# A two-layer hybrid block on one core: squares, a convolution tap and two affine maps from VectorE to ScalarE, and fewer table instructions

## The chip, the core and the metric

The kernel runs on one core of a Trainium2 chip. A core has TensorE (PE in the rows; its weight loads are PEld), VectorE (DVE), ScalarE (ACT), GpSimd (POOL), SyncE (SP), which here issues the transfers, and 16 DMA engines. Each engine works through its own queue of instructions in a fixed order and stops where an instruction has to wait for another engine. The metric is the device time of one execution in microseconds.

## The reference, cut to what matters

Two layers of one trunk run over 512 latent tokens and 256 context tokens of width 1024. In each layer a normalized, modulated input is projected once, its columns are split among three mixers (S5, a complex diagonal state space; gated DeltaNet, GDN; RWKV-7), and the outputs are joined, projected and added. Then comes an MLP with a squared ReLU. The context part of layer 1 has no output and no MLP.

```python
h = rmsnorm(x, norm_mlp[layer]) * (1.0 + sc2) + sh2
x = x + gt2 * (jnp.square(jax.nn.relu(h @ w1)) @ w2)

# GDN: five taps over the sequence, per channel, on the q, k and v columns
qkv = jax.nn.silu(centred_dwconv(p[..., :3 * W], conv_w))

# RWKV-7
k_dir = k[:, :, None, :] * (1.0 + (iclr - 1.0) * k_a)
yn = ((y - mean) * lax.rsqrt(var + RWKV_GN_EPS)).reshape(B, L, RWKV_WIDTH) * ln_w + ln_b

# S5: powers and products of complex numbers, from which the scan's tables are made
a_bar = jnp.exp(A * dt)
coef = (a_bar - 1.0) / A
```

## The kernel before

**Layout and products.** Features lie on the 128 partitions and tokens on the free axis, 512 for the latent part (LAT) and 256 for the context part (CTX). Every large product is made in three fp32r matmuls: the high parts of both operands, the low part of the weight, the low part of the activation (`product`, L296). A block of weights arrives by DMA (`wl`, four buffers), ScalarE rounds it to the high part (L272, `wh`, three buffers), and GpSimd or VectorE subtracts for the low part (L273, `wo`, two buffers); in the LAT MLPs that is GpSimd alone. Activations are split likewise: ScalarE casts (L284), VectorE subtracts (L285).

**Banks.** PSUM results go through named banks. Tag `d`, which the dense products, the convolution and the S5 tables share with other work, has two.

**Stages.** From 0 to some 34 us inputs, weights and modulations are worked on. The S5 tables of layer 0 (`s5_tables`) are begun before the first dense product at 63 us. Then come the input projections of both parts with the convolutions in them (to about 420 us), the GDN and RWKV chains, the S5 mixer, the output projections, the CTX MLP (about 900 to 1300 us) and the LAT MLP of layer 0 (about 1330 to 1960 us, with the tables and some of the input projections of layer 1 between its products). Layer 1's mixers follow, and the last MLP (about 2633 to 2990 us).

**Order.** The order on each engine isn't written out. Code carries priorities (chains first, then reads, preparation, S5, and the dense products), and a scheduler that runs its own timeline sets the order of each queue from these and its own estimates. So an instruction that goes to another engine can move other rows too.

**MLP (`back`).** For each of eight blocks of features, four dense products go to bank `d`; each is read by a ReLU on ScalarE (L1140), squared on VectorE (L1141), cast on ScalarE (L284) and subtracted on VectorE (L285). Then eight products over this block are added to the stream by VectorE (L1150), which frees the bank. There are 96 squares, 64 of 512 columns and 32 of 256.

**Convolution (`conv`).** ScalarE copies the bank into a padded tile (L467), VectorE multiplies the first tap (L470) and adds four more (L472), ScalarE takes the tanh (L473). It runs 33 times. The bank is free when L467 is done.

**Affine maps.** In the RWKV preparation VectorE does `kd * hka + omka` (L1571, 24 times), and in its readout `yc * ln_w + ln_b` (L1749, 9 times).

**Complex products.** `cmul` (L527) makes one of six instructions. `s5_tables` calls it on VectorE for the coefficients, the powers, the tables `f` and, in loops over `p`, for the power table `e` and the squarings whose small tiles have the tag `t5`; later, per group pair, on GpSimd and on VectorE.

Of the kernel before, what the change touches and what calls it, by code (L numbers as in the profile page):

```python
# [11 lines left out]
AF = mybir.ActivationFunctionType  # L12
# [14 lines left out]
        "td": (24, 4), "tp": (24, 4), "tq": (24, 4), "tg": (24, 4), "tr": (24, 4), "t5": (8, 6), "wc": (24, 4),  # L27
# [62 lines left out]
class Kern:  # L90
# [370 lines left out]
    def conv(self, ps, i, n, col):  # L461
# [65 lines left out]
    def cmul(self, eng, o, x, y, t, conj=False):  # L527

        tt = eng.tensor_tensor
        (orr, oi), (xr, xi), (yr, yi), (t0, t1) = o, x, y, t  # L530
        tt(t0, xr, yr, OP.mult)
        tt(t1, xi, yi, OP.mult)
        tt(orr, t0, t1, OP.add if conj else OP.subtract)
        tt(t0, xi, yr, OP.mult)
        tt(t1, xr, yi, OP.mult)
        tt(oi, t0, t1, OP.subtract if conj else OP.add)

    def s5_tables(self, l, col, tags):
# [81 lines left out]
        br, bi = new(), new()  # L620
# [8 lines left out]
        co = (new(), new())  # L629
        self.cmul(v, co, (br, bi), (are, aim), sc[1:3], conj=True)  # L630
        for c in co:
            tt(c, c, q, OP.mult)
        pr, pi = new(9), new(9)
# [4 lines left out]
        t0, t1 = self.s(64), self.s(64)  # L638
        for p in (1, 2, 4):
            sh = lambda a: a[:, :16 * p].rearrange("p (m c) -> p m c", c=16)  # L640
            bc = lambda a: a[:, p:p + 1].to_broadcast([P, p, 16])
            self.cmul(v, (pr[:, p + 1:2 * p + 1], pi[:, p + 1:2 * p + 1]), (pr[:, 1:p + 1], pi[:, 1:p + 1]),
# [12 lines left out]
        wr, wi = new(), new()  # L655
        stt(wr, cm, 1.0, m, OP.add, OP.mult)
        tt(wi, s, m, OP.mult)
# [15 lines left out]
        t = [tw[:, 256 * i:256 * i + 256].rearrange("p (d g c) -> p d g c", d=2, g=8) for i in range(2)]  # L673
        for d in range(2):
            bb = [s5bc[:, 128 * i:128 * i + 128].rearrange("p (g c) -> p g c", c=16) for i in range(2)]
            cc = [c[:, 8 * d:8 * d + 8].unsqueeze(2).to_broadcast([P, 8, 16]) for c in co]
            self.cmul(v, [x[:, d] for x in f], bb, cc, [x[:, d] for x in t])
# [5 lines left out]
        for d in range(2):  # L683
# [8 lines left out]
            ur, ui = wr[:, 8 * d:8 * d + 8], wi[:, 8 * d:8 * d + 8]  # L692
            p = 1
            while p < 96:
# [3 lines left out]
                self.cmul(v, [x[:, :, at(p, p + k)] for x in e], [x[:, :, at(0, k)] for x in e], (bc(ur), bc(ui)), (sh(t0), sh(t1)))  # L698
# [1215 lines left out]
```

## Time and profile before

| | us |
|---|---|
| median of three runs | 3021.07 |
| the three runs | 3020.94, 3021.07, 3024.71 |
| the profiled execution, its own time | 3012.89 |
| its span | 3011.1 |
| TensorE busy | 2663.1 (88%) |
| VectorE busy | 1725.7 (57%) |
| GpSimd busy | 1122.3 (37%) |
| ScalarE busy | 1096.4 (36%) |

The rows are from the profiled execution, which took 8.18 us less than the median of the runs; 1.8 us of its time lie outside the span. A share of busy time is a mean over stages with different limits, so the table alone doesn't tell what a shorter queue on one engine is worth. For that one reads which wait of TensorE ended last, and on whom.

### The profile page before, as it was taken

The page shows a single profiled execution, that of the slowest core. Times are in us where ns is not written, and L with a number is a line of the kernel's source. Part 1 is how long each engine was busy: PE and PEld are TensorE (multiplying, and loading weights), DVE is VectorE, ACT ScalarE, POOL GpSimd, SP SyncE. Part 2 cuts the span into 40 slices and gives each one's busy share as a digit, 9 for nine tenths or more (in the row PEclk, how much of TensorE's full clock was granted, in tenths as well). Part 3 has the DMA queues.
Part 4 walks back from the last instruction along what each step waited for, and adds up shares of the span by engine and source line. Part 5 has one row for each costly group of instructions (what it writes and reads, how often), then busy time and mean ns, then how long its engine had stood idle before and what let it go on. Part 6 is the DMA issues. An engine that isn't in the chain of part 4 may idle for free. (4 is left out here: it accounts for less than half of the span.)

```text
span 3011.1 us, 54432 instructions
## 1 busy us (share of the span) xinstructions
PE 2663.1 (88%) x20052; PEld 2044.2 (68%) x20052; DVE 1725.7 (57%) x4281; ACT 1096.4 (36%) x2250; POOL 1122.3 (37%) x1275
## 2 busy tenths in 40 slices
PE   5889998876899999987889999888888889799998
PEld 2767875653668888776667677667655567478776
DVE  7654875764657667558777543547656453333333
ACT  3344443231434443455323323443323232233332
POOL 2432434433232220323447444344343422244443
PEclk8789998676889999977999999889899768699999
DMA  5345546544645544443344233265466532023322
GB/s 207 95 156 175 153 125 197 158 142 136 206 147 173 141 152 137 147 141 109 88 103 142 94 91 107 90 196 157 135 206 193 163 101 87 29 86 96 95 94 85
DMA packets 324650, 401.65 MB, mean 133 GB/s; under 512 B 142880, under 2 KB 173472, under 8 KB 324384
## 3 DMA queue, kind: packets, MB, share of 16 engines
q1 hardware_dynamic: 324384, 398.18, 43.1%
q8 instruction: 158, 2.59, 0.4%
q14 instruction: 108, 0.88, 0.1%
HBM read 300.70 MB, written 88.90 MB: 129 GB/s over the span
## 5 line engine op out<-in xcount | busy, mean ns | idle before, releaser
L296 PE MATMUL d<-page,wh 128*128 128x512 f32 (+1 forms) x5024 | 1425.3, 367 | 57.3 <-DVE page L1150 22.0
L296 PEld LDWEIGHTS d<-page,wh 128*128 128x128 f32 x5024 | 918.9, 196 | 232.7 <-DVE page L1150 26.6
L296 PE MATMUL d<-page,wo 128*128 128x512 f32 (+1 forms) x2512 | 917.7, 366 | 13.7 <-POOL wo L273 7.4
L273 POOL TENSOR_TENSOR wo<-wl,wh 128x512 fp32r<-128x512 f32 (+1 forms) x357 | 481.0, 1348 | 670.0 <-PE d L296 520.9
L272 ACT CAST wh<-wl 128x512 fp32r<-128x512 f32 (+1 forms) x590 | 360.2, 616 | 553.9 <-PE d L296 391.1
L296 PEld LDWEIGHTS d<-page,wo 128*128 128x128 f32 x2512 | 492.8, 196 | 91.5 <-POOL wo L273 10.7
L273 DVE TENSOR_TENSOR wo<-wl,wh 128x512 fp32r<-128x512 f32 (+1 forms) x233 | 167.4, 720 | 105.1 <-PE d L296 41.5
L1150 DVE SCALAR_TENSOR_TENSOR page<-d,mod,page 128x512 f32<-128x512 f32 (+1 forms) x192 | 124.7, 658 | 161.9 <-PE d L296 161.4
L1141 DVE TENSOR_TENSOR s<-s 128x512 f32<-128x512 f32 (+1 forms) x96 | 82.3, 858 | 158.8 <-ACT s L1140 155.8
L371 DVE TENSOR_TENSOR solve<-solve 128x30 f32<-128x30 f32 (+4 forms) x360 | 138.1, 384 | 53.9 <-issue 46.2
L373 DVE TENSOR_TENSOR solve<-solve 128x30 f32<-128x30 f32 (+4 forms) x360 | 150.7, 419 | 8.0
L1493 POOL TENSOR_TENSOR g<-g,gates 64x128 f32<-64x128 f32 x120 | 59.4, 495 | 185.1 <-DVE g L1498 164.6
L923 PE MATMUL d<-wl,sc 128*32 128x512 f32 x320 | 109.5, 717 | 14.3 <-DMA wl<-in_mod_w_dram 12.8
L285 DVE TENSOR_TENSOR page<-s,page 128x512 fp32r<-128x512 f32 (+1 forms) x118 | 92.4, 785 | 41.5 <-ACT page L284 41.1
L1140 ACT ACTIVATE s<-d 128x512 f32<-128x512 f32 (+1 forms) x96 | 50.6, 527 | 165.8 <-PE d L296 165.6
L284 ACT CAST page<-s 128x512 fp32r<-128x512 f32 (+1 forms) x118 | 64.0, 547 | 92.9 <-DVE s L1141 74.1
L472 DVE SCALAR_TENSOR_TENSOR s<-s,ncol,s 128x512 f32<-128x512 f32 (+1 forms) x132 | 93.8, 713 | 2.8
L1727 PE MATMUL rc<-page,page 128*64 128x64 f32 x464 | 86.0, 273 | 2.0 <-DMA page<-dr 2.0
L1616 PEld LDWEIGHTS p<-page,page 64*128 64x128 f32 x576 | 74.3, 211 | 19.5 <-issue 8.1
L1616 PE MATMUL p<-page,page 64*128 64x128 f32 (+1 forms) x576 | 86.5, 310 | 0.7 <-POOL page L1590 0.7
L1704 DVE TENSOR_TENSOR page<-page,rc 64x128 f32<-64x128 f32 x144 | 40.9, 284 | 78.8 <-PE rc L1702 73.5
L481 PE MATMUL p<-consts,page 128*128 128x128 f32 x348 | 63.7, 306 | 24.6 <-ACT page L1642 9.6
(461 smaller groups left out, 3977.9 us busy)
## 6 DMA issues: line engine op xcount, KB each, us to landing
wl<-in_w_dram SPq DMA_DIRECT2D x384, 256.0 KB, 2.7
wl<-in_mod_w_dram SPq DMA_DIRECT2D x160, 256.0 KB, 3.5
wl<-in_w_in_dram SPq DMA_DIRECT2D x142, 256.0 KB, 3.0
page<-dr SPq DMA_DIRECT2D x118, 256.0 KB, 3.2
dr<-s SPq DMA_DIRECT2D x72, 256.0 KB, 2.6
dr<-page SPq DMA_DIRECT2D x30, 512.0 KB, 4.2
dr<-page SPq DMA_DIRECT2D x55, 256.0 KB, 3.0
page<-dr SPq DMA_DIRECT2D x16, 834.0 KB, 5.0
```

What stands on the lines that cost most here:

```text
L272: nc.scalar.copy(hi, st)
L273: low.tensor_tensor(lo, st, hi.bitcast(F32), OP.subtract)
L285: nc.vector.tensor_tensor(lo, src, hi.bitcast(F32), OP.subtract)
L296: nc.tensor.matmul(ps, x, y, start=(first and i == 0), stop=(last and i == len(order) - 1))
L371: nc.vector.tensor_tensor(tm, y3[:, :j, j:j + 1].to_broadcast([P, j, w]), y3[:, j:j + 1, j + 1:].to_broadcast([P, j, w]), OP.mult)
L373: nc.vector.tensor_tensor(y3[:, :j, j + 1:], y3[:, :j, j + 1:], tm, OP.add)
L472: nc.vector.scalar_tensor_tensor(acc, cp[:, j:j + n], w[:, 5 * i + j:5 * i + j + 1], acc, OP.mult, OP.add)
L923: nc.tensor.matmul(ps[32 * i:32 * i + 32], self.sc[:, k0 + i], t, start=(k0 == 0), stop=(k0 == 4))
L1141: nc.vector.tensor_tensor(r, r, r, OP.mult)
L1150: nc.vector.scalar_tensor_tensor(x[j], ps, mod[:, 40 + j, g:g + 1], x[j], OP.mult, OP.add)
L1616: nc.tensor.matmul(ps[:, i], flat(bk[d][hs, n0 + i]), kr[d][hs, n0 + i], start=True, stop=True)
L1727: nc.tensor.matmul(o, xv[h][:, n, d], self.R[d][:, h, n], start=False, stop=True)
```

## The change

- The 96 squares of the MLP become ScalarE activations (Square) in place.
- The convolution's first instruction on the sum becomes a ScalarE multiply that reads the PSUM bank again with the centre tap; VectorE then adds taps 0, 1, 3 and 4. The bank is read by two ScalarE instructions in place of one.
- The two affine maps become ScalarE activations (Identity) with a scale and a bias per partition.
- `cmul` makes both products of one right part at once, on tiles twice as wide: four instructions in place of six. It is used for the coefficients, the powers, the tables `f` and the `t5` squarings. The old form, `cmul6`, stays for the table `e` and the group pairs.

The diff, cut to its core (the lines that only make the paired tiles are left out):

```diff
-        nc.vector.tensor_scalar(acc, cp[:, 0:n], w[:, 5 * i:5 * i + 1], None, OP.mult)
-        for j in range(1, 5):
+        nc.scalar.mul(acc, ps, w[:, 5 * i + 2:5 * i + 3])
+        for j in (0, 1, 3, 4):
             nc.vector.scalar_tensor_tensor(acc, cp[:, j:j + n], w[:, 5 * i + j:5 * i + j + 1], acc, OP.mult, OP.add)
...
     def cmul(self, eng, o, x, y, t, conj=False):
         tt = eng.tensor_tensor
+        two = lambda z: z.unsqueeze(1).to_broadcast(list(x.shape))
+        a, b = t
+        tt(a, x, two(y[0]), OP.mult)
+        tt(b, x, two(y[1]), OP.mult)
+        tt(o[0], a[:, 0], b[:, 1], OP.add if conj else OP.subtract)
+        tt(o[1], a[:, 1], b[:, 0], OP.subtract if conj else OP.add)
+
+    def cmul6(self, eng, o, x, y, t):
+        tt = eng.tensor_tensor
         (orr, oi), (xr, xi), (yr, yi), (t0, t1) = o, x, y, t
         tt(t0, xr, yr, OP.mult)
         tt(t1, xi, yi, OP.mult)
-        tt(orr, t0, t1, OP.add if conj else OP.subtract)
+        tt(orr, t0, t1, OP.subtract)
         tt(t0, xi, yr, OP.mult)
         tt(t1, xr, yi, OP.mult)
-        tt(oi, t0, t1, OP.subtract if conj else OP.add)
+        tt(oi, t0, t1, OP.add)
...
-                    nr, ni = self.tile('t5', 8), self.tile('t5', 8)
-                    self.cmul(v, (nr, ni), (ur, ui), (ur, ui), (self.tile('t5', 8), self.tile('t5', 8)))
-                    ur, ui = nr, ni
+                    n2, a2, b2 = [self.tile('t5', 16).rearrange("p (x g) -> p x g", x=2) for _ in range(3)]
+                    self.cmul(v, (n2[:, 0], n2[:, 1]), uu, (uu[:, 0], uu[:, 1]), (a2, b2))
+                    uu = n2
...
                             nc.scalar.activation(r, ps, AF.Relu)
-                            nc.vector.tensor_tensor(r, r, r, OP.mult)
+                            nc.scalar.activation(r, r, AF.Square)
...
-                nc.vector.tensor_scalar(kd, kd, col["hka"][:, fc], col["omka"][:, fc], OP.mult, OP.add)
+                nc.scalar.activation(kd, kd, AF.Identity, scale=col["hka"][:, fc], bias=col["omka"][:, fc])
...
-        nc.vector.tensor_scalar(yc, yc, col["ln_w"][:, fc], col["ln_b"][:, fc], OP.mult, OP.add)
+        nc.scalar.activation(yc, yc, AF.Identity, scale=col["ln_w"][:, fc], bias=col["ln_b"][:, fc])
```

Lines move by 10 to 14: L1141 is L1155 after, L1140 is L1154, L930 is L944, L960 is L974. VectorE has 234 rows fewer (4283 to 4049: 162 moved, 72 saved in the tables), ScalarE 162 more (2252 to 2414); TensorE, GpSimd and SyncE have as many as before, and there is no further load of a ScalarE function table. TensorE's rows stand in the same order over the last 1,400, the whole last MLP; over the program 18% of them change places with others.

On VectorE at the program's start the tables of layer 0 (L531 to L536 before, L541 to L546 after) stand with the last modulation (L930, then L944) and the two instructions (L960, then L974) that the first normalized input needs. Before, rows 218 to 229 of the queue:

```order
L533 TENSOR_TENSOR page_18_115<-page_17_113 128x256
L532 TENSOR_TENSOR page_10_99<-page_9_97,t5_107_542 128x32
L532 TENSOR_TENSOR t5_113_560<-t5_107_542 128x8
L930 TENSOR_TENSOR mod_22_132<-d_99_373,cols_20_119 128x8
L536 TENSOR_TENSOR page_19_117<-page_15_109 128x256
L536 TENSOR_TENSOR page_16_111<-page_15_109 128x256
L534 TENSOR_TENSOR page_17_113<-page_17_113,page_14_107 128x256
L535 TENSOR_TENSOR page_17_113<-page_17_113,page_14_107 128x256
L533 TENSOR_TENSOR page_8_95<-page_10_99 128x8x4
L533 TENSOR_TENSOR t5_110_557<-t5_112_559,t5_113_560 128x8
L960 SCALAR_TENSOR_TENSOR ab_174_1059<-mod_22_132,cols_20_119 128x16
L960 SCALAR_TENSOR_TENSOR ab_183_1093<-mod_22_132,cols_20_119 128x16
```

The same place after, rows 207 to 217:

```order
L543 TENSOR_TENSOR page_8_95<-page_10_99 128x8x4
L543 TENSOR_TENSOR page_18_115<-page_17_113 128x256
L944 TENSOR_TENSOR mod_22_132<-d_99_373,cols_20_119 128x8
L546 TENSOR_TENSOR page_19_117<-page_15_109 128x256
L546 TENSOR_TENSOR page_16_111<-page_15_109 128x256
L544 TENSOR_TENSOR page_10_99<-page_9_97,t5_105_526 128x32
L545 TENSOR_TENSOR page_10_99<-page_8_95,t5_105_526 128x32
L544 TENSOR_TENSOR page_17_113<-page_17_113,page_14_107 128x256
L545 TENSOR_TENSOR page_17_113<-page_17_113,page_14_107 128x256
L974 SCALAR_TENSOR_TENSOR ab_162_1011<-mod_22_132,cols_20_119 128x16
L974 SCALAR_TENSOR_TENSOR ab_171_1045<-mod_22_132,cols_20_119 128x16
```

The modulation stood at row 221 and stands at row 209; the pair behind it went from 228 to 216: twelve table instructions fewer stand ahead of both.

On ScalarE in the last MLP, where one block's ReLU, the weight casts (`wh`) and the casts of activations (`page`) follow each other. Before, rows 1899 to 1905:

```order
L1140 ACTIVATE s_4315_27899<-d_4308_27862 128x512
L272 CAST wh_4326_27948<-wl_4325_27947 128x512
L284 CAST page_3846_25557<-s_4315_27899 128x512
L272 CAST wh_4330_27968<-wl_4329_27967 128x512
L1140 ACTIVATE s_4323_27941<-d_4316_27904 128x512
L272 CAST wh_4334_27988<-wl_4333_27987 128x512
L284 CAST page_3847_25559<-s_4323_27941 128x512
```

After, rows 2059 to 2067:

```order
L1154 ACTIVATE s_4291_27803<-d_4284_27766 128x512
L272 CAST wh_4302_27852<-wl_4301_27851 128x512
L1155 ACTIVATE s_4291_27803<-s_4291_27803 128x512
L284 CAST page_3822_25461<-s_4291_27803 128x512
L272 CAST wh_4306_27872<-wl_4305_27871 128x512
L1154 ACTIVATE s_4299_27845<-d_4292_27808 128x512
L272 CAST wh_4310_27892<-wl_4309_27891 128x512
L1155 ACTIVATE s_4299_27845<-s_4299_27845 128x512
L284 CAST page_3823_25463<-s_4299_27845 128x512
```

The square (L1155) stands between the weight cast and the cast of its own result; nothing else moved.

On ScalarE at the convolutions of layer 1's latent part, whose GDN chains (L782, L870, after: L796, L884) run beside the projections. Before, rows 1529 to 1533:

```order
L870 ACTIVATE page_14_107<-page_14_107 128x768
L473 ACTIVATE s_3333_20903<-s_3334_20907 128x512
L467 COPY s_3345_20972<-d_3338_20935 128x512
L272 CAST wh_3364_21065<-wl_3363_21064 128x512
L782 COPY page_717_4005<-d_3349_20995 96x4x64 x2
```

After, rows 1652 to 1657:

```order
L884 ACTIVATE page_14_107<-page_14_107 128x768
L796 COPY page_705_3957<-d_3324_20892 96x4x64 x2
L467 COPY s_3321_20876<-d_3314_20839 128x512
L470 ACTIVATE s_3322_20880<-d_3314_20839,ncol_24_135 128x512
L272 CAST wh_3340_20969<-wl_3339_20968 128x512
L796 COPY page_705_3957<-d_3325_20899 96x4x64 x2
```

The multiply (L470) follows its copy at once and stands ahead of the next weight cast, and the bank `d` that both read is free one instruction later.

## Rows read from the trace of the kernel before

**Rows 1.** The page, first part: busy time, share of the span and instructions.
```profile
PE 2663.1 (88%) x20052; PEld 2044.2 (68%) x20052; DVE 1725.7 (57%) x4281; ACT 1096.4 (36%) x2250; POOL 1122.3 (37%) x1275
```

**Rows 2.** Windows: stretch, its us, busy PE (matmuls) PEld DVE ACT POOL, clock, DMA, GB/s.
```profile
1320.00:1962.00 642.00, 571.81 (x3316) 445.04 (x3317) 398.77 (x846) 244.71 (x490) 294.20 (x313) 0.91 0.36 107
2600.00:3011.00 411.00, 384.63 (x1642) 307.95 (x1640) 149.80 (x178) 133.08 (x223) 181.21 (x136) 0.97 0.28 89
```

**Rows 3.** Chain of waits, last MLP: start, us, engine, tile, line (one of seven pairs).
```profile
2707.51 0.76 DVE page L1150
2708.32 44.01 PE d L296 x191
```

**Rows 4.** Last MLP, timeline: start, us, engine, line, operation [idle before, releaser].
```profile
2663.47 0.50 PE L296 MATMUL d<-page,wh 128*128 128x512 f32 x1 [0.62 <-DVE page L1150]
...
2702.24 0.60 ACT L1140 ACTIVATE s<-d 128x512 f32<-128x512 f32 x1 [2.07 <-PE d L296]
...
2702.87 1.19 DVE L1141 TENSOR_TENSOR s<-s 128x512 f32<-128x512 f32 x1 [2.92 <-ACT s L1140]
...
2704.10 0.62 ACT L284 CAST page<-s 128x512 fp32r<-128x512 f32 x1 [0.75 <-DVE s L1141]
```

**Rows 5.** Lines by form: busy us, mean ns | idle before, releasers.
```profile
L1141 DVE TENSOR_TENSOR s<-s 128x512 f32<-128x512 f32 x64 | 67.9, 1060 | 158.6 <-ACT s L1140 155.8 <-issue 2.8
L1140 ACT ACTIVATE s<-d 128x512 f32<-128x512 f32 x64 | 38.3, 598 | 133.0 <-PE d L296 133.0
L939 ACT ACTIVATE s<-page 128x512 f32<-128x512 f32 x40 | 24.1, 625 | 9.3 <-DVE page L1150 7.0 <-DMA dr<-s 0.5 <-DVE s L943 0.3
L1063 ACT ACTIVATE s<-q,ncol 128x512 f32<-128x512 f32 x24 | 15.6, 684 | 10.2 <-PE q L1061 7.5 <-issue 2.6
L512 ACT ACTIVATE s<-s,ncol 128x512 f32<-128x512 f32 x24 | 17.4, 724 | 55.3 <-DMA s<-s 55.0 <-ACT page L1408 0.3
L1141 DVE TENSOR_TENSOR s<-s 128x256 f32<-128x256 f32 x32 | 14.5, 452 | 0.1
L1140 ACT ACTIVATE s<-d 128x256 f32<-128x256 f32 x32 | 12.3, 384 | 32.7 <-PE d L296 32.6
L470 DVE TENSOR_SCALAR s<-s,ncol 128x512 f32<-128x512 f32 x18 | 9.8, 547 | 4.0 <-ACT s L467 4.0
```

**Rows 6.** Waits of PE, 1320 to 1962 us: us, times, longest.
```profile
PE d L296 <- DVE page L1150: 14.1, 12, 4.1
```

**Rows 7.** Layer-0 LAT MLP, timeline: a square and the cast behind it.
```profile
1522.99 0.69 DVE L1141 TENSOR_TENSOR s<-s 128x512 f32<-128x512 f32 x1
...
1523.71 0.62 ACT L284 CAST page<-s 128x512 fp32r<-128x512 f32 x1 [4.09 <-DVE s L1141]
```

**Rows 8.** Start: window of 30 to 62 us, then two rows of the timeline.
```profile
30.00:62.00 32.00, 22.07 (x118) 9.77 (x118) 27.56 (x182) 4.68 (x14) 9.14 (x12) 0.76 0.44 164
...
59.77 0.15 DVE L930 TENSOR_TENSOR mod<-d,cols 128x8 f32<-128x8 f32 x1
...
63.22 0.58 PE L296 MATMUL d<-page,wh 128*128 128x256 f32 x1 [2.00 <-ACT page L974]
```

**Rows 9.** Whole span, waits of PE: us, times, longest.
```profile
PE d L946 <- DVE s L943: 27.3, 5, 14.7
...
PE d L296 <- DVE page L1150: 22.0, 25, 4.1
...
PE d L440 <- DVE s L427: 13.8, 4, 4.3
...
PE d L839 <- ACT s L467: 3.9, 1, 3.9
...
PE d L296 <- ACT s L467: 3.5, 3, 1.7
```

**Rows 10.** Lines asked for: count, ns min/median/max, first and last start, forms.
```profile
L1571 DVE TENSOR_SCALAR page<-page,ncol x24: 399/490/1093, 230.6 to 2364.4; 128x256 f32<-128x256 f32 x12, 128x512 f32<-128x512 f32 x12
...
L1749 DVE TENSOR_SCALAR page<-page,cols x9: 412/545/1145, 470.9 to 2595.7; 128x512 f32<-128x512 f32 x6, 128x256 f32<-128x256 f32 x3
```

More of the change, by code (lines that the diff above doesn't have):

```diff
@@ L619, in s5_tables @@
         s, cm = double(*double(s, cm))
-        br, bi = new(), new()
+        bri = new(2)
+        br, bi = bri[:, 0], bri[:, 1]
         tt(br, ex, cm, OP.mult)
@@ L628, in s5_tables @@
         v.reciprocal(q, q)
-        co = (new(), new())
-        self.cmul(v, co, (br, bi), (are, aim), sc[1:3], conj=True)
+        co = new(2)
+        self.cmul(v, (co[:, 0], co[:, 1]), bri, (are, aim), (new(2), new(2)), conj=True)
+        co = [co[:, i] for i in range(2)]
         for c in co:
             tt(c, c, q, OP.mult)
-        pr, pi = new(9), new(9)
+        pw = new(18).rearrange("p (c m) i -> p c m i", c=2)
+        pr, pi = pw[:, 0], pw[:, 1]
         v.memset(pr[:, 0], 1.0)
@@ L654, in s5_tables @@
         ts(m, m, -0.5, 1.0, OP.mult, OP.add)
-        wr, wi = new(), new()
-        stt(wr, cm, 1.0, m, OP.add, OP.mult)
-        tt(wi, s, m, OP.mult)
+        wri = new(2)
+        stt(wri[:, 0], cm, 1.0, m, OP.add, OP.mult)
+        tt(wri[:, 1], s, m, OP.mult)
         keep = self.s(768, keep=kept)
@@ L672, in s5_tables @@
         tw = self.s(512)
-        t = [tw[:, 256 * i:256 * i + 256].rearrange("p (d g c) -> p d g c", d=2, g=8) for i in range(2)]
+        t = [tw[:, 256 * i:256 * i + 256].rearrange("p (x g c) -> p x g c", x=2, g=8) for i in range(2)]
         for d in range(2):
-            bb = [s5bc[:, 128 * i:128 * i + 128].rearrange("p (g c) -> p g c", c=16) for i in range(2)]
+            bb = s5bc[:, 0:256].rearrange("p (x g c) -> p x g c", x=2, c=16)
             cc = [c[:, 8 * d:8 * d + 8].unsqueeze(2).to_broadcast([P, 8, 16]) for c in co]
-            self.cmul(v, [x[:, d] for x in f], bb, cc, [x[:, d] for x in t])
+            self.cmul(v, [x[:, d] for x in f], bb, cc, t)
         cr = s5bc[:, 256:512].rearrange("p (g c) -> p g c", c=32)
@@ L697, in s5_tables @@
                 bc = lambda a: a.unsqueeze(2).to_broadcast([P, 8, k])
-                self.cmul(v, [x[:, :, at(p, p + k)] for x in e], [x[:, :, at(0, k)] for x in e], (bc(ur), bc(ui)), (sh(t0), sh(t1)))
+                self.cmul6(v, [x[:, :, at(p, p + k)] for x in e], [x[:, :, at(0, k)] for x in e],
+                           (bc(uu[:, 0]), bc(uu[:, 1])), (sh(t0), sh(t1)))
                 p += k
                 if p < 96:
-                    nr, ni = self.tile('t5', 8), self.tile('t5', 8)
-                    self.cmul(v, (nr, ni), (ur, ui), (ur, ui), (self.tile('t5', 8), self.tile('t5', 8)))
-                    ur, ui = nr, ni
+                    n2, a2, b2 = [self.tile('t5', 16).rearrange("p (x g) -> p x g", x=2) for _ in range(3)]
+                    self.cmul(v, (n2[:, 0], n2[:, 1]), uu, (uu[:, 0], uu[:, 1]), (a2, b2))
+                    uu = n2
             for c in range(2):
@@ L720, in s5_tables @@
                 ej = lambda a: a[:, :, gp].unsqueeze(3).to_broadcast(shape)
-                self.cmul(nc.gpsimd, (qr, qi), [ej(a) for a in drv],
-                          [a[:, :, gp].unsqueeze(2).to_broadcast(shape) for a in f], (t0, t1))
-                self.cmul(v, (pr, pi), [ej(a) for a in rdo],
-                          [a[:, gp, 0:16].unsqueeze(1).unsqueeze(1).to_broadcast(shape) for a in (cr, ci)], (t2, t3))
+                self.cmul6(nc.gpsimd, (qr, qi), [ej(a) for a in drv],
+                           [a[:, :, gp].unsqueeze(2).to_broadcast(shape) for a in f], (t0, t1))
+                self.cmul6(v, (pr, pi), [ej(a) for a in rdo],
+                           [a[:, gp, 0:16].unsqueeze(1).unsqueeze(1).to_broadcast(shape) for a in (cr, ci)], (t2, t3))
                 pq = bank().rearrange("p (d c n) -> p d c n", d=2, c=2)
```

10 lines of the change are left out of this document (5 added, 5 removed).

## The prediction

> **What bounds the kernel now.** I read the busy shares first. TensorE is busy for 88% of the span and VectorE for 57% [rows 1], so an engine that isn't the bound gets lighter, and what that is worth must be read from the moments at which TensorE stood still for VectorE. The windows come next: in the layer-0 LAT MLP (1320 to 1962 us) TensorE is busy for 571.81 of 642 us, in the stage with the last MLP for 384.63 of 411 [rows 2]. Then the chain of waits in the last MLP: each of its blocks is 44.01 us of matmuls and 0.76 us of one residual addition, and neither ReLU nor square is in it [rows 3]. Last, the list of TensorE's waits: 27.3 us in five waits on a normalization (L943), 22.0 us in 25 on the MLP's residual (L1150), 13.8 us in four on L427, and only 7.4 us (3.9 and 3.5) on the convolution's copy [rows 9]. The reader is to see that many small waits, and no single one, hold what can be won or lost.
>
> **What VectorE sheds and ScalarE takes.** Squares: 67.9 + 14.5 = 82.4 us. First taps: 18 took 9.8 us at 0.547; the other 15 have half the columns and I count them at 0.40, 6.0 us [rows 5]; together 15.8. Affine maps: 24 x 0.490 + 9 x 0.545 = 16.7 [rows 10]. Table instructions: 72 fewer, and in the stretch in which those of layer 0 run 182 instructions took 27.56 us, 0.151 us each [rows 8], so 10.9. The sum is 125.8 us, 7.3% of VectorE's 1725.7. ScalarE takes 64 squares at 0.625 (the nearest row is L939, an activation from SBUF to SBUF of the same size), 32 at 0.384 (the ReLU of 256 columns), 33 multiplies at up to 0.684 (L1063 reads PSUM with one column operand) and 33 affine maps at up to 0.724 (L512, SBUF with one column operand) [rows 5]: 40.0 + 12.3 + 22.6 + 23.9 = 98.8 us at most, 9% on its 1096.4. At some 40% of the span it would then stand above GpSimd and well below VectorE (53%).
>
> **Part A, the squares.** In the last MLP I cost them at nothing. The square ran from 2702.87 to 2704.06 and the cast followed at 2704.10 [rows 4]. Afterwards ScalarE's weight cast stands between ReLU and square (the ordered rows of the last MLP): 0.60 of ReLU from 2702.24, a weight cast of some 0.6 us, a square of 0.625 give 2704.06 again. The cover is the next dense product's 24 matmuls, far longer than this chain; if it were gone, the price would be the difference just worked out, near zero. The gap of 0.62 us at the turn of two blocks [rows 4] is the bank's release by L1150 and stays, since TensorE's order there is the same. In the layer-0 LAT MLP there is more to win: the cast waited 4.09 us for a square that took 0.69 [rows 7], because the square stood in VectorE's queue behind work of layer 1's tables and chains. TensorE's waits on L1150 there are 14.1 us in 12 [rows 6]. Eight turns of blocks at about 0.65 us are the bank again, 5 us; the other 9 us come from VectorE's queue. The squares take 32 x 1.06 = 34 us of the 398.77 that VectorE is busy there [rows 2, 5], so its queue is a tenth shorter, and each chain that ends in such a wait loses one place in that queue. I take -4, with 0 and -9 as ends.
>
> **Part B, layer 0's tables.** The first dense product starts at 63.22 us, 2.00 us after TensorE was free, released by ScalarE's L974, which follows the last modulation at 59.77 (L930) and the two instructions behind it [rows 8]. In VectorE's queue twelve table instructions fewer stand ahead of these: 12 x 0.151 = 1.8 us. I take -2. The ends are 0 (weights or another load are next) and -5.4 (36 instructions saved per layer, all ahead).
>
> **Part C, layer 1's tables.** The same 36 instructions run beside the MLP, where VectorE is seldom last: -1, from 0 to -5.4.
>
> **Part D, the convolution.** Bank `d` has two buffers and is now held for one instruction more, at most 0.684 us. What hides it is the other bank's dense product. TensorE waited on L467 in four places, 7.4 us [rows 9]; there the hold comes on top, 4 x 0.684 = 2.7. In exchange VectorE's four additions begin about as early as before (a multiply of 0.684 for one of 0.547). A weight cast waits behind each multiply on ScalarE, as the ordered rows at layer 1's convolutions show, and TensorE behind that. I take +2; the ends are 0 and 33 x 0.684 = +22.6, if nothing hides it anywhere. A gain from this step isn't excluded, but it is VectorE's shorter queue, which part F counts.
>
> **Part E, the affine maps.** Each goes from VectorE to ScalarE between two neighbours that stay (a VectorE multiply behind L1571, a GpSimd addition behind L1749), so a chain gets one or two more changes of engine. At 0.724 for 0.490 the price is 0.234 each, 7.7 us for all 33; most lie beside dense products or other chains. I take +1, between 0 and +8.
>
> **Part F, VectorE's queue elsewhere.** Waits of TensorE on VectorE outside the MLP are led by 27.3 and 13.8 us [rows 9], 41 us. Most of a normalization is its own chain of operations, not a queue. A queue 7% shorter gives back a tenth of these waits: -4, from 0 to -20 (half of them). The scheduler's new order, which changes places for 18% of TensorE's rows, has no sign that I can read; it widens the range by some 10 us both ways.
>
> **The sum:** 0 - 4 - 2 - 1 + 2 + 1 - 4 = -8 us. On the profiled execution's 3012.89 that is 3004.9. This execution was 8.18 us under the median of 3021.07, so against the median I forecast 3021.07 - 8 = 3013.
>
> **A rule that speaks against the change.** The rows show that a multiply by a column costs 0.547 us on VectorE and 0.684 to 0.724 on ScalarE for 512 columns, while a square costs 1.060 on VectorE and 0.625 on ScalarE [rows 5]. The Trainium skill (ScalarE: Activation LUTs, Rules for kernel authors) tells authors to keep additions and multiplications on VectorE; by that rule the taps and the affine maps are a step back, and the rows agree with it for these two and not for the squares. The same page (What ACT_TABLE_LOAD costs) prices two column operands at an estimated 0.80 us for 512 columns (186 + 2 x 93 + 0.833 x 512 ns), which no row of before shows; part E's upper end would be +10 by it in place of +8.
>
> **Rivals.**
> 1. *No change.* The relieved engine isn't the bound: every square, tap and map lay under matmuls, TensorE's 2663.1 us stay, and the waits on VectorE that count are serial chains (27.3 us in five waits, longest 14.7). For it: the chain of the last MLP has none of the moved lines [rows 3]. Against it: the queueing in [rows 6, 7]. Time: 3021, from 3015 to 3027.
> 2. *Slower: ScalarE's queue holds the banks.* The multiply stands ahead of the next weight cast and keeps a bank of `d`. It decides where the weight cast or the bank, and not VectorE, is what TensorE waits for: layer 1's projections, which run beside chains that use the same bank and engine. If half of the 33 multiplies are exposed, that is 11.3 us; affine maps at the upper end, 7.7; and the gains shrink to B and part of A, -5. Together +14: 3035. For it: TensorE already waited 3.9 us once for L467 in front of L839 and three times in front of a dense product [rows 9]. Against it: these waits are four of 33.
> 3. *Larger gain.* The queue waits vanish: A -9, B -5, C -3, F -12, D +2, E +1 make -26: 2995. For it: VectorE has the widest spread of waits. Against it: removing 7% of an engine's work seldom removes all waits on it.
> 4. *The scheduler undoes it*, by placing other rows so that the lighter engine starts something later. It has no time of its own and lies in the 10 us above.
>
> **Chances.** The forecast (6 to 20 us faster) 0.39, the larger gain 0.11, no change 0.27, slower 0.23. A measurement of this kernel tells a change from none at about 0.2%, 6 us. So faster 0.50, same 0.27, slower 0.23. The range goes from 2994 (the larger gain's price) to 3034 (just short of the slower rival's), which leaves about one in ten on each side.
>
> **What would show it.** Right, if VectorE is busy for about 1600 us and ScalarE for 1180 to 1195; if the first dense product starts near 61.4; if TensorE's waits on the residual in the layer-0 LAT MLP fall from 14.1 to about 10; if a block of the last MLP still takes 44.8 us; if its waits on the convolution's two ScalarE lines are about 10 us in place of 7.4. Wrong on the slow side, if these are 15 or more, or if waits on weight casts grow where convolutions run. Wrong altogether, if the chains of layer 1 start or end elsewhere by more than 10 us, which would be the scheduler's order and none of the parts.

## The result

The changed kernel took 3004.32 us in the median of nine runs (2996.11 to 3013.7), the kernel before 3022.5 us in nine runs beside it (3018.79 to 3025.75). The ratio is 0.9943, with an interval of 0.9924 to 0.9962: about 17 us faster. The forecast was 3013 us, in a range of 2994 to 3034.

The first rows are of the page of the changed kernel: the span, and the busy time, share and instructions of each engine.

```profile
span 2995.7 us, 54437 instructions
...
PE 2671.5 (89%) x20052; PEld 2050.0 (68%) x20052; DVE 1584.1 (53%) x4047; ACT 1176.4 (39%) x2412; POOL 1104.4 (37%) x1275
```

Against [rows 1], VectorE has 141.6 us less to do (the sum said 125.8) and ScalarE 80.0 more (at most 98.8). TensorE is the engine to look at: span less busy time is its idle time, 3011.1 - 2663.1 = 348.0 us before and 324.2 after. It stood still for 23.8 us less. But the same 20052 matmuls took 8.4 us longer. The gain of 15.4 us in the span is the difference of the two, and the second number was in none of the prediction's terms.

The rows below are the windows of the changed kernel (stretch, length, busy PE PEld DVE ACT POOL with their counts, granted clock, DMA share, GB/s): the start, the two MLP stages, and then the layer-0 chains, the CTX stage, the layer-0 LAT MLP and layer 1. The last four are cut at the same dense products in every kernel, matmuls 1256, 1413, 3454, 4710 and 5966 of the 7536 of L296, counted from 0, so their lengths can be compared.

```profile
30.00:62.00 32.00, 23.40 (x118) 10.22 (x118) 26.99 (x170) 4.71 (x14) 9.09 (x12) 0.78 0.44 161
1320.00:1962.00 642.00, 580.11 (x3375) 449.95 (x3375) 355.85 (x777) 280.95 (x551) 295.03 (x316) 0.91 0.38 115
2600.00:3011.00 411.00, 369.38 (x1585) 296.21 (x1583) 95.53 (x136) 143.51 (x244) 173.83 (x131) 0.97 0.27 86
...
426.81:819.21 392.40, 333.77 (x3144) 228.62 (x3142) 226.74 (x708) 130.00 (x292) 143.59 (x182) 0.77 0.55 167
819.21:1338.76 519.55, 484.24 (x4604) 408.73 (x4603) 312.90 (x786) 239.31 (x518) 121.33 (x153) 0.93 0.47 148
1338.76:1764.03 425.27, 385.22 (x2530) 299.74 (x2529) 274.09 (x648) 182.99 (x369) 209.28 (x229) 0.91 0.37 110
1764.03:2596.60 832.57, 736.25 (x5863) 534.11 (x5862) 394.16 (x979) 291.27 (x572) 308.50 (x346) 0.82 0.43 133
```

The same four stages in the kernel before:

```profile
432.65:825.92 393.27, 322.50 (x3120) 220.94 (x3119) 236.52 (x712) 124.36 (x281) 146.48 (x182) 0.78 0.55 165
825.92:1346.56 520.64, 487.94 (x4635) 412.20 (x4634) 327.41 (x835) 226.19 (x480) 122.39 (x153) 0.93 0.48 148
1346.56:1785.80 439.24, 387.24 (x2531) 298.86 (x2529) 306.80 (x710) 164.33 (x336) 212.37 (x230) 0.92 0.36 106
1785.80:2611.77 825.97, 727.32 (x5864) 528.04 (x5862) 422.23 (x1005) 276.57 (x546) 314.31 (x346) 0.85 0.44 135
```

In the chains of layer 0 TensorE's idle time (length less busy) fell from 70.8 to 58.6 us, but its busy time rose from 322.5 to 333.8, and the stage is 0.9 us shorter. In the LAT MLP idle fell from 52.0 to 40.1 us and busy hardly moved: 14 us won. In layer 1 the stage is 6.6 us longer at a clock of 0.82 in place of 0.85. The rest was won ahead of the chains: 369.4 us from the first dense product before (63.22 to 432.65), 363.3 after (63.54 to 426.81).

How far can one profiled execution be trusted with such differences? `p_sq`, the kernel before with the squares alone moved, has the kernel before's rows on every queue until its first square at 907 us. Its two stages ahead of that take 4.6 us less and 4.7 us more than before:

```profile
63.09:427.91 364.82, 333.45 (x2177) 266.82 (x2177) 248.55 (x606) 158.68 (x353) 137.23 (x198) 0.89 0.45 141
427.91:825.88 397.97, 328.86 (x3119) 224.27 (x3118) 236.25 (x712) 124.67 (x281) 145.94 (x182) 0.77 0.54 164
```

Four kernels share these rows (before, `p_sq`, `sq_lat`, `sq_rest`). In the layer-0 chains they took 393.3 to 399.8 us, with TensorE busy for 322.5 to 328.9 and idle for 69.0 to 72.2. The changed kernel and `m_sq` (the changed kernel with the squares back) have one order up to 901 us, and took 392.4 and 403.9 us there, busy 333.8 and 341.3, idle 58.6 and 62.6. So a stage can differ by 5 to 12 us with not one instruction moved, most of it in busy time. The 6.1 us ahead of the chains are within that (`m_sq` took 368.2 us there), and idle time is the steadier number.

In the LAT MLP TensorE's waits on the residual are these (us, times, longest), against 14.1 in [rows 6]:

```profile
PE d L296 <- DVE page L1164: 9.5, 8, 3.9
```

The last MLP has the old block: chain of waits (start, us, engine, tile, line), as [rows 3].

```profile
2691.85 0.76 DVE page L1164
2692.66 44.00 PE d L296 x191
```

And within a block, on the timeline, the square (L1155) stands between a weight cast and its own cast, which starts 1.67 us after the ReLU did, against 1.86 in [rows 4]:

```profile
2686.59 0.60 ACT L1154 ACTIVATE s<-d 128x512 f32<-128x512 f32 x1 [2.08 <-PE d L296]
2687.08 0.61 ACT L272 CAST wh<-wl 128x512 fp32r<-128x512 f32 x1
2687.59 0.63 ACT L1155 ACTIVATE s<-s 128x512 f32<-128x512 f32 x1
2688.26 0.62 ACT L284 CAST page<-s 128x512 fp32r<-128x512 f32 x1
```

### The profile page after: what moved, and what is told of

Same layout as the page of the kernel before. It is cut to its first block, busy times and chain, and to the rows that moved or that the text cites. A ratio compares the mean times of both kernels' runs of the same rounds, so it can differ in the third digit from the quotient of the medians.

```text
span 2995.7 us, 54437 instructions
## 1 busy us (share of the span) xinstructions
PE 2671.5 (89%) x20052; PEld 2050.0 (68%) x20052; DVE 1584.1 (53%) x4047; ACT 1176.4 (39%) x2412; POOL 1104.4 (37%) x1275
## 5 line engine op out<-in xcount | busy, mean ns | idle before, releaser
L296 PE MATMUL d<-page,wh 128*128 128x512 f32 (+1 forms) x5024 | 1421.0, 366 | 49.3 <-DVE page L1164 18.8
L296 PEld LDWEIGHTS d<-page,wh 128*128 128x128 f32 x5024 | 919.2, 196 | 220.9 <-DVE page L1164 25.2
L296 PE MATMUL d<-page,wo 128*128 128x512 f32 (+1 forms) x2512 | 916.6, 365 | 11.5 <-DVE wo L273 7.7
L273 POOL TENSOR_TENSOR wo<-wl,wh 128x512 fp32r<-128x512 f32 (+1 forms) x357 | 475.3, 1332 | 653.0 <-PE d L296 528.5
L272 ACT CAST wh<-wl 128x512 fp32r<-128x512 f32 (+1 forms) x590 | 360.4, 615 | 567.9 <-PE d L296 411.7
L296 PEld LDWEIGHTS d<-page,wo 128*128 128x128 f32 x2512 | 493.1, 196 | 87.3 <-DVE wo L273 10.4
L273 DVE TENSOR_TENSOR wo<-wl,wh 128x512 fp32r<-128x512 f32 (+1 forms) x233 | 168.2, 723 | 135.5 <-PE d L296 61.4
L285 DVE TENSOR_TENSOR page<-s,page 128x512 fp32r<-128x512 f32 (+1 forms) x118 | 78.6, 669 | 260.4 <-ACT page L284 260.2
L937 PE MATMUL d<-wl,sc 128*32 128x512 f32 x320 | 110.6, 750 | 13.8 <-DMA wl<-in_mod_w_dram 12.0
L1154 ACT ACTIVATE s<-d 128x512 f32<-128x512 f32 (+1 forms) x96 | 50.6, 527 | 163.8 <-PE d L296 163.4
L472 DVE SCALAR_TENSOR_TENSOR s<-s,ncol,s 128x256 f32<-128x256 f32 (+1 forms) x132 | 90.9, 694 | 20.0 <-ACT s L470 16.3
L1498 DVE TENSOR_TENSOR g<-page,gc 64x128 f32<-64x128 f32 x144 | 40.8, 283 | 82.6 <-PE gc L1496 62.0
L1740 PE MATMUL rc<-page,r 64*64 64x64 f32 x432 | 78.7, 268 | 3.1 <-DVE r L1732 1.8
L481 PEld LDWEIGHTS p<-consts,page 128*128 128x128 f32 x348 | 43.0, 155 | 42.3 <-issue 13.3
```

What stands on the lines that cost most here:

```text
L272: nc.scalar.copy(hi, st)
L273: low.tensor_tensor(lo, st, hi.bitcast(F32), OP.subtract)
L296: nc.tensor.matmul(ps, x, y, start=(first and i == 0), stop=(last and i == len(order) - 1))
L481: self.nc.tensor.transpose(p[:, t * 128:(t + 1) * 128], src[:, t * 128:(t + 1) * 128], self.ident)
L937: nc.tensor.matmul(ps[32 * i:32 * i + 32], self.sc[:, k0 + i], t, start=(k0 == 0), stop=(k0 == 4))
L1740: nc.tensor.matmul(o, st[hs, d], kr[d][hs, n, 1], start=True, stop=False)
```

## The experiments

Three theories stood against each other. Q: VectorE's queue gets shorter, and TensorE's waits with it, part by part as in the sum. O: the scheduler's new order decides, whatever was moved. L (and S): the squares alone are the change, in one stage or another. The kernels are each part alone, each part undone, the squares in two halves, and two kernels with one trivial instruction more. The table puts the results together: each ratio is to runs of the kernel before on the same chip (medians 3019.11 to 3022.5 us), and "idle" is the profiled span less TensorE's busy time, from each kernel's page. Each page is one execution: that of before took 8.2 us less than its median, those of the others between 6.8 us less (the changed kernel) and 6.8 us more (`m_aff`).

| kernel | what it has | median us | ratio to before (interval) | PE busy | PE idle |
|---|---|---|---|---|---|
| before | nothing | 3021.07 | | 2663.1 | 348.0 |
| `p_sq` | squares | 3006.59 | 0.9950 (0.9928 to 0.9971) | 2655.0 | 345.4 |
| `p_conv` | convolution | 3039.15 | 1.0065 (1.0045 to 1.0085) | 2677.3 | 364.7 |
| `p_aff` | affine maps | 3024.90 | 1.0023 (1.0001 to 1.0045) | 2672.0 | 357.4 |
| `p_tab` | tables | 3025.03 | 1.0014 (0.9992 to 1.0036) | 2670.8 | 353.0 |
| `sq_lat` | layer-0 LAT squares | 3019.73 | 1.0003 (0.9983 to 1.0024) | 2677.2 | 341.3 |
| `sq_rest` | other squares | 3005.45 | 0.9952 (0.9929 to 0.9975) | 2647.0 | 357.2 |
| `n_tiny` | nothing, and a tiny instruction | 3022.43 | 0.9998 (0.9972 to 1.0025) | 2681.0 | 344.1 |
| `m_sq` | all but squares | 3016.16 | 0.9980 (0.9953 to 1.0007) | 2685.6 | 334.4 |
| `m_conv` | all but convolution | 3017.53 | 0.9986 (0.9963 to 1.0009) | 2681.6 | 338.5 |
| `m_aff` | all but affine maps | 3029.84 | 1.0030 (1.0008 to 1.0052) | 2696.9 | 338.0 |
| `m_tab` | all but tables | 3023.22 | 0.9993 (0.9968 to 1.0018) | 2686.5 | 341.0 |
| `n_after` | all, and a tiny instruction | 3017.87 | 0.9981 (0.9958 to 1.0004) | 2682.2 | 333.2 |
| after | all | 3004.32 | 0.9943 (0.9924 to 0.9962) | 2671.5 | 324.2 |

**Each part alone.** The squares alone, on the kernel before:

```diff
-                            nc.vector.tensor_tensor(r, r, r, OP.mult)
+                            nc.scalar.activation(r, r, AF.Square)
```

> The kernel before with the 96 squares alone on ScalarE. Theory Q (VectorE's queue gets shorter, by the parts of the prediction): part A's -4 us and two thirds of part F's -4, so -7 us on the median of before; TensorE's waits on the MLP's residual between 1320 and 1962 us fall from 14.1 us to about 10, and nothing changes before the CTX MLP begins at about 900 us. Theory O (the scheduler's new order is what counts, not the load moved): a change between -10 and +10 us of any sign, spread over stretches in which no square stands. Theory S (the squares are the whole change): -17 to -18 us.

They gave 0.9950, some 15 us, twice what theory Q expected. It looked like the whole change, as theory S said. TensorE's waits on the residual fell to 10.6 us, as theory Q had named. But TensorE is idle for only 2.6 us less than before, and busy for 8.1 us less: the gain is of the other kind than the changed kernel's.

```diff
-        nc.vector.tensor_scalar(acc, cp[:, 0:n], w[:, 5 * i:5 * i + 1], None, OP.mult)
-        for j in range(1, 5):
+        nc.scalar.mul(acc, ps, w[:, 5 * i + 2:5 * i + 3])
+        for j in (0, 1, 3, 4):
```

> The kernel before with the convolution's first instruction alone on ScalarE. Theory Q: part D's +2 us less 0.5 us of part F: +1.5 us, with some 10 us of waits of TensorE on the two ScalarE lines of the convolution. Theory O: between -10 and +10 us. A third reading, from the trace of the changed kernel, where 5.8 us were won between 63 and 430 us, the stretch of the first projections and convolutions: -5 to -6 us by this part alone, won before 430 us.

1.0065: about 20 us slower, twice the end of theory O's range, and none of it in the stage where 18 of the 33 multiplies run: 369.4 us from the first dense product to the 1256th before, 368.4 (63.86 to 432.25) here. TensorE waits for the convolution's two ScalarE lines for 4.4 us here and 7.4 before [rows 9]. The loss is in the two chain stages, in which no convolution (layer 0) or nine of 33 (layer 1, 16.3 us longer) run. The first of them, from `p_conv`'s windows, 17.5 us longer than before:

```profile
432.25:842.97 410.72, 332.38 (x3126) 226.51 (x3126) 236.05 (x712) 125.39 (x284) 145.20 (x181) 0.77 0.53 159
```

```diff
-                nc.vector.tensor_scalar(kd, kd, col["hka"][:, fc], col["omka"][:, fc], OP.mult, OP.add)
+                nc.scalar.activation(kd, kd, AF.Identity, scale=col["hka"][:, fc], bias=col["omka"][:, fc])
```

(and the same for `yc` in the readout)

> The kernel before with the two affine maps alone on ScalarE. Theory Q: part E's +1 us less 0.5 us: about 0 us. Rival (the chains pay each change of engine): +8 us. Theory O: between -10 and +10 us.

1.0023, just clear of no change. The tables alone were the changed kernel's `cmul`, its callers and `cmul6`, with everything else as before:

> The kernel before with the four-instruction complex products alone. Theory Q as predicted: parts B and C, -3 us, with the first dense product at 61.4 us in place of 63.2. The trace of the changed kernel shows that product at 63.5 us, so part B should give 0 here too and the whole -1 us. Theory O: between -10 and +10 us. If this part brings what was won between 63 and 430 us: -6 us by then.

1.0014, not told from no change. VectorE was busy for 1722.0 us in it, 3.7 less than before, where 10.9 had been counted. The four ratios add up to some 16 us slower; the four parts together are 17 us faster. The parts don't add up.

**Each part undone.** The edits are those above, backwards, on the changed kernel.

> The changed kernel with the squares back on VectorE. Measured alone, the squares gave 0.995, the convolution 1.0065, the affine maps 1.0023 and the tables 1.0014, which add up to about +16 us where the whole change gave -17. Theory Q (the squares take waits off the MLP whatever the rest does): 12 to 15 us slower than the changed kernel, so 3017 to 3020 us, lost between 1340 and 1800 us. Theory O (the scheduler's order decides): anything from -20 to +20 us against the changed kernel, lost or won in stretches without squares.

> The changed kernel with the convolution's first tap back on VectorE. If the parts add up, it sheds the +20 us that this part cost alone: 2985 us, better than both. Theory O: the +20 us was the order of the chains between 430 and 830 us, which this part redrew, and not the multiply; then taking it back brings no such gain, and the time is between 2995 and 3025 us.

> The changed kernel with the two affine maps back on VectorE. If the parts add up: 7 us faster than the changed kernel, 2997 us. Theory O: between 2985 and 3025 us, with the difference in the chains between 430 and 830 us or after 2100 us.

> The changed kernel with the six-instruction complex products throughout. Theory Q: the tables were worth at most 3 us and showed +6 us alone, so 2998 to 3007 us. Theory O (any undoing redraws the chains' order, and each of the three so far came out 11 to 26 us slower): 3012 to 3030 us.

All four came out 12 to 26 us slower than the changed kernel in the median, `m_sq` with an interval that overlaps the changed kernel's. The convolution cost 20 us alone and its removal costs 13 us; the affine maps cost 6 us alone and their removal 26. A cost that belonged to the instruction would keep its sign. `m_conv` and `m_aff`, and the two parts alone, refute adding up; `m_tab` refutes theory Q's 2998 to 3007 us for the tables. `m_sq` is not told apart by its median (12 us, at the edge of theory Q), but it kept the short LAT MLP without a single square on ScalarE: 424.93 us, as the changed kernel's 425.27.

```profile
1356.62:1781.55 424.93, 379.01 (x2531) 292.77 (x2529) 297.97 (x669) 167.81 (x345) 215.00 (x226) 0.94 0.38 110
```

**An instruction that does nothing.** To the kernel before, and later to the changed one, one line was added ahead of the convolution's sum, a multiplication of one column by 1.0:

```diff
+        nc.vector.tensor_scalar(cp[:, 2:3], cp[:, 2:3], 1.0, None, OP.mult)
         acc = self.d(n)
```

> The kernel before with one more VectorE instruction of a single column (a multiplication by 1.0) in each of the 33 convolutions and nothing moved to another engine. Its own cost is at most 33 x 0.15 us (a small table instruction), 5 us on VectorE, most of it hidden. But about as many rows of TensorE's order change places as by the whole change. Theory Q: 0 to +2 us against before. Theory O: a difference of the size that the parts showed, 5 to 20 us of either sign, made in the chains.

VectorE's busy time is 0.9 us longer than before, but from 142 us on, where the first convolutions run, TensorE's order is another one (in `p_conv` from 139 us). The median didn't move (0.9998), against theory O for the whole; the stages did. The layer-0 chains of `n_tiny`, with the convolution's arithmetic as before, are as long as those of `p_conv`:

```profile
431.07:843.17 412.10, 336.13 (x3135) 229.03 (x3134) 238.72 (x712) 124.92 (x283) 148.41 (x182) 0.76 0.53 158
```

18.8 us were lost there against before, and part of it came back in the LAT MLP and layer 1 (821.49 us for the last of the four stages, against 825.97 before). So a stage as long as `p_conv`'s needs no multiply. But executions with the same rows differ by up to 12 us here, so the order's share is better read from idle time: 76.0 us in `n_tiny` and 78.3 in `p_conv`, against 69.0 to 72.2 in the four kernels with the order of before. In `n_tiny` that is some 4 to 7 us by a new order alone. That the order did it in `p_conv` too is argued from this, not shown.

> The changed kernel with one more VectorE instruction of a single column in each of the 33 convolutions. In the kernel before the same addition redrew the order and left the time at 0.9998 (0.9972 to 1.0025). If the changed kernel's gain is in its parts: within 5 us of it, 3000 to 3010 us. If its gain beyond the squares (-17 against -14) and beyond its neighbours with one part undone (3016 to 3030 us) is a lucky order: 3012 to 3025 us.

3017.87 us, 13.5 above the changed kernel in the median, in the range for a lucky order. The two intervals overlap by a hair (0.9958 and 0.9962), so it is probable and not certain. Of all the runs, only this one and `n_tiny` test the order with no load moved.

**The squares in two halves.** The condition stands in front of the two forms of the square, `l == 0 and part is LAT` for the first and its opposite for the second.

> The kernel before with the 32 squares of the layer-0 LAT MLP alone on ScalarE. TensorE's order ahead of that MLP is the one of before. Theory Q: the MLP stage (dense products 3454 to 4710) has some 7 us less idle time of TensorE, as the kernels with squares on ScalarE had so far (40.0 to 46.9 us against 45.9 to 54.6), so -7 us on the median, some of it given back in layer 1's chains. Theory L (the squares' -14 us came from the order that they redrew in the CTX stage and the chains): within 3 us of before.

> The kernel before with the other 64 squares, of the CTX MLP and the last MLP, on ScalarE. Theory Q: 0 in the last MLP (its blocks keep 44.8 us), up to -5 us in the CTX stage: -2 to -5 us. If Q holds for both, this and the LAT squares add up to the -14 us of all 96; theory L puts most of the -14 us here, in the stage between 830 and 1350 us.

1.0003 for the LAT squares and 0.9952 for the others: together what all of them gave, and all of it from the half of which the prediction expected nothing. The LAT MLP with its squares on ScalarE, and the waits on its residual (L1153 in this kernel):

```profile
1348.91:1789.49 440.58, 385.87 (x2530) 299.96 (x2529) 275.90 (x686) 178.46 (x361) 211.72 (x230) 0.92 0.36 106
```

```profile
PE d L296 <- DVE page L1153: 16.0, 10, 4.9
```

VectorE is busy there for 31 us less than before, as meant, and TensorE waits for the residual for 16.0 us where it waited for 14.1. The longest of these waits ends behind five table instructions in a row on VectorE (L534, L535, L536, L531, L532). The stage is 1.3 us longer. In `sq_rest` the CTX stage is 6.9 us shorter than before:

```profile
827.41:1341.16 513.75, 479.24 (x4636) 406.00 (x4634) 320.54 (x804) 234.00 (x511) 121.78 (x154) 0.94 0.49 150
```

`p_sq`, which has the same order of TensorE up to here, has 512.78 us; `sq_lat`, with the order of before, 522.01 against 520.64. So in this stage kernels with one order agree within 1.4 us, and the squares of the CTX MLP, with the order that came with them, are worth some 7 to 8 us in these two kernels. In others they are not: the changed kernel with these squares takes 519.5 us here and `m_sq` without them 520.5, and over the seven kernels with them the stage takes 508.1 to 525.2 us, over the seven without 516.9 to 524.6. TensorE's idle time there rose by 1.8 us in `sq_rest` (32.7 to 34.5); it is the busy time that is 8.7 us shorter, at a granted clock of 0.94 in place of 0.93. No kernel here has these squares and the old order, so which of the two it was stays open. Of the 14 us between the medians of `sq_rest` and before, the two profiled spans show 6.9, because the profiled execution of before lay 8.2 us under its median; over the whole span TensorE is busy for 16.1 us less and idle for 9.2 us more. The clock goes with it: `sq_rest`'s twelve executions were granted 0.886 on the mean, the 35 of before beside them 0.881.

None of the twelve beats the changed kernel; `p_sq` and `sq_rest` equal it with a fraction of the edit.

## Why the prediction was right, and where it wasn't

The range held, the sign was right, and the time was 9 us below the forecast. But few of the eight microseconds are where the sum had put them, and that the forecast's own case came out was in part luck: with one empty instruction more the same edit measured 3017.87 us, which is the first rival's time (3015 to 3027).

Of the signs that the prediction named, the residual's waits (9.5 us for 10) and the blocks of the last MLP came true, VectorE (1584.1 us) and ScalarE (1176.4) came close, and the first dense product and the convolution's waits did not. The sign for "wrong altogether" came true as well: layer 1's stage starts 21.8 us earlier and ends 15.2 us earlier. It can't tell the order from the parts, since whatever is won ahead of layer 1 moves it too.

**Part A, last MLP: right.** Eight blocks of 44.8 us, and the last 1570 dense matmuls took 381.7 to 382.7 us in every one of the fourteen kernels.

**Part A, LAT MLP: the step failed, though what it named as its sign came true.** The residual's waits fell to 9.5 us, "about 10" as forecast. The step that failed is the one from [rows 7] to [rows 6]: a square that stood in VectorE's queue made a cast late, and from that I concluded that the residual's waits came from the same queueing and would fall with the squares. `sq_lat` took the squares away and the waits stayed; `m_sq` kept the squares and the stage was as short as the changed kernel's. The shortest waits of all are in `p_aff`, which keeps every square on VectorE:

```profile
PE d L296 <- DVE page L1150: 8.8, 8, 3.1
```

Over the fourteen kernels the waits are 9.5 to 16.0 us with these squares on ScalarE (mean 11.6) and 8.8 to 15.1 without (mean 12.6): 1 us, where 4 had been put down. TensorE's whole idle time in the stage is 4.7 us shorter on the mean (46.2 against 50.9, with `sq_lat` and `m_sq` against the rule), so some of the gain may be the squares' by another wait; that isn't shown. The long waits on the residual end behind table and solve instructions in VectorE's queue, and where these stand is the order. A signal that agrees with the forecast in the changed kernel alone can't tell the two apart; the half change could.

**Part A, CTX MLP: left out.** The prediction costed squares of 512 columns in two LAT stages and said nothing of the 32 in the CTX MLP. `p_sq` and `sq_rest` are 7 to 8 us shorter in that stage; the changed kernel itself is 1.1 us shorter there.

**Part B: mis-sized.** The first dense product starts at 63.54 us, not 61.4. The last modulation (L944) and this product on the timeline, as in [rows 8]:

```profile
60.10 0.15 DVE L944 TENSOR_TENSOR mod<-d,cols 128x8 f32<-128x8 f32 x1
...
63.54 0.58 PE L296 MATMUL d<-page,wh 128*128 128x256 f32 x1 [1.81 <-ACT page L988]
```

From 34 us on, 171 instructions up to this modulation kept VectorE busy for 25.49 us before, and 160 for 25.24 us after, with 0.6 us more idle time between them. Eleven fewer, at 0.15 us each, should have saved 1.7. The term was a mean price times a count; but the four instructions that are left do the work of the six on tiles twice as wide. In the six kernels with the tables the first dense product starts at 62.9 to 64.0 us, in the eight without at 63.1 to 63.9. Over the program `p_tab` saved 3.7 us of VectorE's time in 72 instructions, 0.05 us each.

**Part C** can't be told apart; the tables' own ratio allows -2 to +11 us.

**Part D: too high by itself.** TensorE's waits on the convolution's ScalarE lines are 3.5 us after, where 10 had been expected and 7.4 stood before:

```profile
PE d L853 <- ACT s L470: 2.7, 1, 2.7
PE d L296 <- ACT s L470: 0.8, 1, 0.8
```

The bank that is held for 0.70 us longer wasn't the next thing waited for. The part's price alone was that of the slower rival's size (20 us), but not by the rival's mechanism, which needed these waits to grow. The rival's other sign, waits on weight casts (L272), is 17.9 us in `p_conv` for 12.5 before; but `n_tiny`, which moves no multiply, has 16.0, and the changed kernel 6.8.

**Part E.** Its direct price was as feared, one map of 512 columns at 0.809 us, and the part alone was 0 to 14 us slower by its interval.

**Part F: the step failed, though idle time fell by more than it forecast.** The waits on VectorE that the part named are L943's and L427's, 27.3 and 13.8 us [rows 9]. After, the first stands where it stood and the second lost one wait of four:

```profile
PE d L960 <- DVE s L957: 27.3, 5, 14.7
PE d L440 <- DVE s L427: 11.3, 3, 4.3
```

TensorE's whole idle time fell by 23.8 us, when everything that the sum gave came to 8. And it isn't the one profile: in the six kernels with three or four of the parts TensorE was idle for 334.9 us on the mean (324.2 to 341.0), in the eight with one or none for 351.4 (341.3 to 364.7). But a shorter queue on VectorE doesn't explain it. Summed over each kernel's list of waits, those that the traces put down to VectorE are 154.8 us on the mean in the six and 156.0 in the eight; the changed kernel, with 139.4, is alone at the low end (the other thirteen, before among them with 156.0: 152.1 to 168.9). The 16 us are in waits put down to ScalarE (86.8 against 95.2 us), GpSimd (36.3 against 41.0) and others. Nor does idle time follow VectorE's load: `m_sq`, where VectorE is busy for 1687.7 us, is idle for 334.4, and `p_sq`, with 1629.9, for 345.4. What the parts have in common that shortens idle time stays open.

**The term that was missing.** In the same six kernels TensorE's busy time is 2684.1 us on the mean, in the eight 2667.9: 16 us more for the same matmuls. What went from idle time is there in busy time, and the mean ratios of the two groups, 0.9986 and 1.0001, are only some 4.5 us apart. Shown is that the two go together over fourteen profiles, and that the granted clock, a mean over each kernel's runs, goes with it (0.8783 in the six, 0.8811 in the eight). Single executions of one kernel show the clock's part too: of the 35 of before beside `n_after`, the eight that were granted 0.878 or less took 3030.0 us on the mean, the six with 0.884 or more 3015.4. Which way the link runs (a shorter wait that costs clock, or a slower matmul that covers more of a wait) and why the clock is granted less was not tried, and stays open.

**The order.** The prediction gave the scheduler's redrawing 10 us both ways and no sign. That may be the largest thing in the case: the layer-0 chains alone took 390 to 422 us in the fourteen kernels. The changed kernel has one of the shortest (392.4), and that it beats its neighbours with one part less, or with one empty instruction more, by 12 to 26 us is best read as a good draw in part. It isn't shown: `n_tiny` redrew the order and left the median where it was, and that the parts don't add up would also follow if they acted on each other. Single executions also differ: `m_sq` has the changed kernel's order on all engines through the first quarter of TensorE's rows, and still was 3.1 us later at the first solve of a chain (L366) and 11.5 us longer in the layer-0 chains. So only medians of many runs, and stages that several kernels share, carry the argument.

## What to carry to other kernels

Where a scheduler draws the order, a part's worth is not the difference of two kernels: add an instruction that does nothing and see how far the median and the stages move, before a gain or a loss is put down to the edit. See first how far a stage moves between executions whose instructions are the same up to there. A wait that is shorter in the changed kernel isn't yet a wait that the edit shortened; make half of the edit and look at the same wait. And read TensorE's gain as two numbers, idle time and busy time for the same matmuls: the changed kernel won in idle time and lost in busy time, `sq_rest` the other way round, and their medians are 1 us apart.

## What the runs showed of the hardware

Lines by form (busy us, mean ns | idle before, releasers), first of the changed kernel:

```profile
L285 DVE TENSOR_TENSOR page<-s,page 128x512 fp32r<-128x512 f32 x78 | 60.9, 784 | 256.3 <-ACT page L284 256.1
L1155 ACT ACTIVATE s<-s 128x512 f32<-128x512 f32 x64 | 40.5, 633 | 0.1
L470 ACT ACTIVATE s<-d,ncol 128x512 f32<-128x512 f32 x18 | 12.5, 697 | 0.0
L1585 ACT ACTIVATE page<-page,ncol 128x512 f32<-128x512 f32 x12 | 9.7, 809 | 7.8 <-DVE page L1584 7.2 <-DMA s<-s 0.5
```

and of the kernel before:

```profile
L285 DVE TENSOR_TENSOR page<-s,page 128x512 fp32r<-128x512 f32 x78 | 72.6, 932 | 40.5 <-ACT page L284 40.1 <-PE d L296 0.3
```

VectorE's subtraction (L285), which the change doesn't touch, takes 784 ns where it took 932: 12 us of VectorE's lower load come from that alone. The square itself took 0.69 and 1.19 us in different places before [rows 4, 7]. The rows of the last MLP show what differs, GpSimd's subtraction (L273) beside VectorE's. Before:

```profile
2688.48 1.30 POOL L273 TENSOR_TENSOR wo<-wl,wh 128x512 fp32r<-128x512 f32 x1 [1.22 <-PE d L296]
2688.49 1.84 DVE L285 TENSOR_TENSOR page<-s,page 128x512 fp32r<-128x512 f32 x1 [0.69 <-ACT page L284]
```

After, where VectorE starts first:

```profile
2672.66 0.69 DVE L285 TENSOR_TENSOR page<-s,page 128x512 fp32r<-128x512 f32 x1 [7.29 <-ACT page L284]
2672.82 1.68 POOL L273 TENSOR_TENSOR wo<-wl,wh 128x512 fp32r<-128x512 f32 x1 [1.22 <-PE d L296]
```

It holds throughout: over the fourteen traces, the 847 of these subtractions that started while no GpSimd instruction was running took 695 ns at most, the 273 that started while one was running 1331 ns on the mean. And it is the move of the last MLP's squares that changes it there: from 2500 us on the mean is 692 to 693 ns in all seven kernels with these squares on ScalarE, 919 to 987 in the seven without. The Trainium skill (SBUF — State Buffer, Who interferes with whom) says that a VectorE instruction with two SBUF operands and a GpSimd instruction that reads SBUF exclude each other; the trace agrees, though no run here took the GpSimd work away. This price is also in the squares' mean of 1.060 us [rows 5], by which the prediction counted what VectorE sheds.

The two column operands of the affine map cost 809 ns for 512 columns, where the prediction's estimate from the Trainium skill (ScalarE: Activation LUTs, What ACT_TABLE_LOAD costs) was 0.80 us: the trace agrees.
